# Two of the four weight sums of a down pair: from VectorE additions to accumulating loads issued by GpSimd

## The chip, the cores and the metric

The kernel runs on one core of a Trainium2 chip. The metric is the device time of the program in microseconds. Before the change it is 1649.35 us, the median of three runs (1645.39, 1649.7 and 1649.35). The profiled execution, from which every row below comes, took 1654.24 us.

## The reference

Two layers of a hybrid encoder run on 544 tokens (512 of a first chunk and 32 of a later one) with shared weights. Each layer has two kinds of attention, a cross-attention to 256 memory tokens, and an MLP. The change touches only the second half of the MLP:

```python
hm = rmsnorm(x, norm_mlp[l])                       # x: 544 x 1024
x = x + jnp.square(jax.nn.relu(hm @ w_up[l])) @ w_down[l]   # w_up: 1024 x 4096, w_down: 4096 x 1024
```

Everything is float32, and the kernel keeps that precision by splitting every operand into a high part and a rest (`h` and `lo`) and forming three products.

## The kernel before

The MLP of a layer is done in four groups. A group takes 1024 of the 4096 hidden columns: first eight dense "up" blocks (PE multiplies, VectorE and ScalarE turn the results into activations and their sums), then four "down pairs", each with 128 output rows of the lower and of the upper half of the model width, so a 2 x 2 arrangement of blocks of `w_down` (W11, W21, W12, W22) against the two halves of the tokens and hidden columns. A pair is computed with a Strassen-Winograd scheme: seven products instead of eight, for which four sums of weight blocks are needed besides the four blocks.

`pair()` (line 330) gives each pair its five steps. `load` takes a buffer of seven blocks of 128 x 512 from a ring of two and loads 1 MB in two transfers of 512 KB on SP's queue (line 337). `add(n)` (line 342) is one VectorE addition of 128 x 512. `split(u)` (lines 352 and 353) rounds one or two blocks on ScalarE and subtracts on VectorE; it writes to rings of two (`uh`, `ul`: two blocks) and three (`wh`, `wl`: one block). `product(n)` (line 368) is 12 matmuls. `evac(n)` (line 1085, `evac_pair`) is one VectorE addition that puts a product's PSUM bank on the residual. The sums and the places of the buffer are:

```python
W11, S1, W12, W22, S3, S2, S4 = range(7)
W21 = S1
UNITS = ((W11, 2), (S2, 2), (W12, 1), (S3, 1), (W22, 1))
o, a, b = ((S3, W11, W21), (S1, W21, W22), (S2, S1, W11), (S4, S2, W12))[n]
```

So add 0 is S3 = W11 + W21, add 1 turns W21 in its own place into S1 = W21 + W22, add 2 is S2 = S1 + W11, add 3 is S4 = S2 + W12. Unit 0 (W11 and S1) feeds a pair's first products, unit 1 (S2 and S4) the next.

The order of the 28 products of a group is the table `GROUP`: 0 to 27, with the products of neighbouring pairs interleaved. Products 0, 1, 4, 5, 6, 7, 10 belong to the group's pair 0; 2, 3, 8, 9, 11, 12, 15 to pair 1; 13, 14, 16 to 19, 22 to pair 2; and 20, 21, 23 to 27 to pair 3. Within a pair, the products Q1, N6, Q7 and P4 go to one PSUM bank one after the other, and each is added to what is there, so PE may start Q7 (7, 12, 19, 26) only when VectorE has read the bank after N6 (4, 8, 16, 23), and P4 (10, 15, 22, 27) only after the evacuation of Q7. The pairs take turns in two PSUM buffers, so that pair 2 starts (13) when pair 0's P4 (10) has been read.

`plan()` decides behind which product each load, addition and split is written. The buffer of pair i is free for pair i + 2 when the last split of pair i has been read by VectorE. `mlp()` places the additions of the first two pairs of a group among the up blocks. The tile framework then gives each engine its own order, in which additions and evacuations can change places; the order that counts is the built one, shown with the change.

Of the kernel before, what the change touches and what calls it, by code (L numbers as in the profile page):

```python
# [12 lines left out]
ALU = mybir.AluOpType  # L13
# [41 lines left out]
W11, S1, W12, W22, S3, S2, S4 = range(7)  # L55
W21 = S1
# [32 lines left out]
class Program:  # L89
# [240 lines left out]
    def pair(self, ap, evac):  # L330
# [2 lines left out]

        def load():
            w = st["w"] = self.mlp_pool.tile([128, 7, 512], F32, tag="quad", name="w", bufs=2)
            for c, o in ((0, W11), (1, W12)):
                self.nc.sync.dma_start(out=w[:, o:o + 2].rearrange("p s c -> p (s c)"), in_=ap[c])

        def add(n):
            o, a, b = ((S3, W11, W21), (S1, W21, W22), (S2, S1, W11), (S4, S2, W12))[n]  # L340
            w = st["w"]
            self.nc.vector.tensor_tensor(w[:, o], w[:, a], w[:, b], ALU.add)  # L342

# [1072 lines left out]
    def mlp(self, l, A, goff, bind, at, behind):  # L1416
# [3 lines left out]
        for grp in range(4):  # L1420
            up = [self.dense(io["w_up"][l, 8 * grp + j], 128, *A, bind(self.evac_up, j),
                             ahead=int(n < 7 and (n or not grp))) for n, j in enumerate(PAIRED)]
# [16 lines left out]
        for grp, (up, down) in enumerate(groups):  # L1439
            p0 = HP * grp  # L1440
# [3 lines left out]
            for n in range(8):  # L1444
                j = PAIRED[n]
                late = 2 if grp == 0 and n == 0 else 0
                if n < 7:
                    up[n + 1] = at(up[n + 1], 5 + late, self.rest_up)
                    up[n + 1] = at(up[n + 1], 2 + late, self.sums_up, j)

                if n:
                    up[n] = at(up[n], 8, call, p0 + n // 5, "add", (n - 1) % 4)
                if n == 7:
                    up[n] = at(up[n], 9, call, p0 + 1, "add", 3)
                    up[n] = at(up[n], 1, call, p0, "split", 0)
                    up[n] = at(up[n], 5, call, p0 + 1, "split", 0)
            if grp:
# [15 lines left out]
            for q, (i, n) in enumerate(prods):  # L1473
# [5 lines left out]
                if q:  # L1479
                    i, n = prods[q - 1]  # L1480
                    do(pairs[p0 + i]["evac"], n)
            i, n = prods[q1 - 1]
# [22 lines left out]
    def plan(self, prods, p0, call):  # L1505

        use, free, todo = {}, {}, {}
        for q, (i, n) in enumerate(prods):
            use.setdefault((i, PRODUCTS[n][0]), []).append(q)

        def when(q, i, *a):
            todo.setdefault(q, []).append((call, p0 + i) + a)

        for rank, (ring, units, ahead) in enumerate(RINGS):
            order = sorted((k for k in use if k[1] in units), key=lambda k: use[k][0])
            for n, (i, u) in enumerate(order):
                q = max(use[order[n - ring]][-1] + 1 if n >= ring else 0, use[i, u][0] - ahead)
                assert q < use[i, u][0] or (i, u) == (0, 0)
                free[i] = max(free.get(i, 0), q)
                if u or i > 1:  # L1520
                    todo.setdefault(q + 0.5, []).append((call, p0 + i, "split", u))
        for i in range(HP):
            when(free[i] + 0.7, i + 2, "load")
        for i in (2, 3):
            a, b = [use[i, u][0] - 5 for u in (0, 1)]
            for k, q in enumerate((a - 1, a, b - 1, b)):
                when(max(q, free[i - 2] + 3), i, "add", k)
        return {q: [f for k in sorted(todo) if int(k) == q for f in todo[k]] for q in range(len(prods))}

    def run(self):  # L1530
# [130 lines left out]
```

## Time and profile before

| | |
|---|---|
| median of three runs | 1649.35 us |
| profiled execution: time, and span of its instructions | 1654.24 us, 1652.3 us |
| PE busy | 1602.4 us, 97% of the span |
| VectorE (DVE), ScalarE (ACT), GpSimd (POOL) busy | 1110.5, 800.2 and 313.5 us |
| granted TensorE clock, mean | 0.989 |
| moved by DMA | 157.22 MB, mean 95 GB/s |

The two MLPs take from about 425 to 830 us and from about 1235 us to the end. A line of the timeline is start, duration, engine, source line, operation, output and inputs; in brackets stands the idle time of that engine just before it and the work whose end released it. Rows of neighbouring instructions overlap a little: an engine starts the next when the last one's write is still under way, so the distance between starts is what one costs.

### The profile page before, as it was taken

The numbers are of one execution on the slowest core, as the hardware profiler recorded it, in microseconds if no ns is written. First come the engines' busy times: TensorE is split into PE (matmuls) and PEld (weight loads), VectorE is DVE, ScalarE is ACT, GpSimd is POOL, SyncE is SP. The second block draws the span as 40 slices with busy tenths as digits, with TensorE's granted clock in tenths as the row PEclk, the third lists the DMA queues.
The fourth block names the chain that finished last, engine by engine and source line by source line (L and its number), as shares of the span: only waits on it lengthen the run. The fifth ranks groups of instructions, "written<-read, shape, count | busy, mean of one in ns | idle before, by whom it ended". The sixth has DMA issues, their size and how long they took to land.

```text
span 1652.3 us, 30168 instructions
## 1 busy us (share of the span) xinstructions
PE 1602.4 (97%) x12159; PEld 1512.4 (92%) x12159; DVE 1110.5 (67%) x2135; ACT 800.2 (48%) x1545; POOL 313.5 (19%) x299
## 2 busy tenths in 40 slices
PE   9899999999999999999998999999999999999996
PEld 8777899998999999999987778999989999999996
DVE  6956674355668777776867556634567686867776
ACT  6655564444454444434446555544444434444453
POOL 3524233421300000000244223334212000000003
PEclk9999999999999999999999999999999999999999
DMA  5313156222432223232123112553233223232312
GB/s 164 100 44 110 57 164 175 90 77 68 128 90 90 92 88 103 77 115 74 51 84 101 58 63 89 160 160 90 78 102 91 77 88 105 90 102 78 115 39 80
DMA packets 56395, 157.22 MB, mean 95 GB/s; under 512 B 6768, under 2 KB 16048, under 8 KB 56256
## 3 DMA queue, kind: packets, MB, share of 16 engines
q1 hardware_dynamic: 55984, 155.02, 30.0%
q8 instruction: 95, 1.56, 0.4%
q14 instruction: 44, 0.36, 0.1%
q10 hardware_dynamic: 272, 0.28, 0.0%
HBM read 143.49 MB, written 11.75 MB: 94 GB/s over the span
## 4 chain that ended last, share of the span: by engine, by line
PE 79%; DVE 10%; DMA 4%; ACT 2%; POOL 1%; issue 1%; DVEq 0%; SPq 0%; POOLq 0%; ACTq 0%
PE pd L299 53%; PE pd L368 11%; DMA w<-w_down 2%; PE pw L368 2%; PE pt L474 1%; PE S L641 1%; PE S L573 1%; PE pv L668 1%; PE pv L527 1%; DVE XG L1085 1%; DVE ul L353 1%; PE S L572 1%; PE pv L587 1%; PE S L509 1%; DVE w L342 1%; PE pd L977 1%
## 5 line engine op out<-in xcount | busy, mean ns | idle before, releaser
L299 PE MATMUL pd<-Ah,wl 128*128 128x272 f32 (+2 forms) x2032 | 458.9, 297 | 8.9 <-DVE wl L269 5.4
L299 PE MATMUL pd<-Ah,wh 128*128 128x272 f32 (+2 forms) x2032 | 441.0, 288 | 1.6 <-ACT Ah L410 1.6
L299 PE MATMUL pd<-Al,wh 128*128 128x272 f32 (+2 forms) x2032 | 439.4, 287 | 0.1
L266 ACT CAST wh<-raw 128x512 fp32r<-128x512 f32 (+1 forms) x362 | 221.9, 615 | 303.2 <-PE pd L299 227.1
L299 PEld LDWEIGHTS pd<-Ah,wl 128*128 128x128 f32 (+1 forms) x2032 | 328.7, 189 | 21.7 <-issue 9.6
L299 PEld LDWEIGHTS pd<-Ah,wh 128*128 128x128 f32 (+1 forms) x2032 | 327.8, 189 | 3.1 <-ACT Ah L410 2.6
L299 PEld LDWEIGHTS pd<-Al,wh 128*128 128x128 f32 (+1 forms) x2032 | 328.8, 189 | 0.3 <-DVE Al L411 0.3
L426 POOL TENSOR_TENSOR acc<-acc,sq 128x544 f32<-128x544 f32 x45 | 69.2, 1538 | 806.7 <-ACT sq L425 806.5
L269 DVE TENSOR_TENSOR wl<-raw,wh 128x512 fp32r<-128x512 f32 (+1 forms) x260 | 185.7, 714 | 53.2 <-ACT wh L266 50.8
L269 POOL TENSOR_TENSOR wl<-raw,wh 128x512 fp32r<-128x512 f32 (+1 forms) x102 | 133.2, 1307 | 339.1 <-ACT wh L266 221.3
L352 ACT CAST wh<-w 128x512 fp32r<-128x512 f32 x96 | 59.5, 619 | 142.1 <-PE pw L368 62.0
L299 PE MATMUL pd<-Bh,wl 128*128 128x272 f32 (+1 forms) x576 | 124.4, 295 | 0.7 <-POOL wl L269 0.5
L299 PE MATMUL pd<-Bh,wh 128*128 128x272 f32 (+1 forms) x576 | 121.1, 290 | 0.0
L299 PE MATMUL pd<-Bl,wh 128*128 128x272 f32 (+1 forms) x576 | 121.1, 289 | 0.0
L342 DVE TENSOR_TENSOR w<-w 128x512 f32<-128x512 f32 x128 | 93.2, 730 | 35.7 <-DMA w<-w_down 35.2
L352 ACT CAST uh<-w 128x1024 fp32r<-128x1024 f32 x64 | 67.2, 1051 | 79.3 <-DVE w L342 60.9
L299 PEld LDWEIGHTS pd<-Bh,wl 128*128 128x128 f32 x576 | 90.7, 188 | 3.5 <-issue 1.0
L299 PEld LDWEIGHTS pd<-Bl,wh 128*128 128x128 f32 x576 | 91.1, 189 | 0.3
L299 PEld LDWEIGHTS pd<-Bh,wh 128*128 128x128 f32 x576 | 90.6, 188 | 0.5
L1085 DVE TENSOR_TENSOR XG<-XG,pd 128x272 f32<-128x272 f32 x192 | 80.5, 433 | 13.6 <-PE pd L368 11.8
L353 DVE TENSOR_TENSOR ul<-w,uh 128x1024 fp32r<-128x1024 f32 x64 | 78.1, 1220 | 2.4 <-ACT uh L352 2.4
L1141 DVE SCALAR_TENSOR_TENSOR up<-pd,R 128x544 f32<-128x544 f32 x64 | 46.2, 722 | 45.7 <-PE pd L299 45.7
(309 smaller groups left out, 3219.4 us busy)
## 6 DMA issues: line engine op xcount, KB each, us to landing
w<-w_down SPq DMA_DIRECT2D x64, 512.0 KB, 4.5
raw<-w_up SPq DMA_DIRECT2D x64, 512.0 KB, 3.6
raw<-w_in SPq DMA_DIRECT2D x28, 512.0 KB, 3.4
raw<-w_mk SPq DMA_DIRECT2D x16, 512.0 KB, 3.9
raw<-w_mv SPq DMA_DIRECT2D x16, 512.0 KB, 3.9
raw<-w_out SPq DMA_DIRECT2D x16, 512.0 KB, 3.7
raw<-w_xq SPq DMA_DIRECT2D x16, 512.0 KB, 3.6
raw<-w_xo SPq DMA_DIRECT2D x16, 512.0 KB, 3.6
```

The lines of the kernel that those rows point to most:

```text
L266: nc.scalar.copy(h[:, :n], r)
L269: eng.tensor_tensor(lo[:, :n], r, h[:, :n].bitcast(F32), ALU.subtract)
L299: nc.tensor.matmul(o, w, a[:, c0:c1], start=start and n == 0, stop=stop and n == 2)
L342: self.nc.vector.tensor_tensor(w[:, o], w[:, a], w[:, b], ALU.add)
L352: self.nc.scalar.copy(h, r)
L353: self.nc.vector.tensor_tensor(lo, r, h.bitcast(F32), ALU.subtract)
L368: self.nc.tensor.matmul(st[bank], w[:, c], a, start=first and i == 0 and m == 0, stop=i == HP - 1 and m == 2, skip_group_check=True)
L426: nc.gpsimd.tensor_tensor(self.acc, self.acc, sq, ALU.add)
L474: nc.tensor.transpose(pt[:, j], P[:, j * 128:(j + 1) * 128], self.ident)
L509: nc.tensor.matmul(ps[:, :w], q[hh][:r, i * 128:n], k[hh][:r, :w], start=m == 0, stop=m == 1)
L1085: self.nc.vector.tensor_tensor(x, x, ps, op)
L1141: nc.vector.scalar_tensor_tensor(halves(t), ps[:, :, :HALF], 0.0, halves(self.R), ALU.max, ALU.mult)
```

## The change

W21 is loaded twice, into its own place and into that of S3. Two transfers issued by GpSimd with an addition on the way then put W11 on the second copy (S3) and W22 on the first (S1). VectorE keeps S2 and S4. W21 and W11 are fetched by transfers of 256 KB of their own, W12 and W22 stay in one of 512 KB.

```diff
         def load():
             w = st["w"] = self.mlp_pool.tile([128, 7, 512], F32, tag="quad", name="w", bufs=2)
-            for c, o in ((0, W11), (1, W12)):
-                self.nc.sync.dma_start(out=w[:, o:o + 2].rearrange("p s c -> p (s c)"), in_=ap[c])
+            w11, w21, w12, w22 = [ap[c][:, k:k + 512] for c in range(2) for k in (0, 512)]
+            for o, src in ((S3, w21), (W21, w21)):
+                self.nc.sync.dma_start(out=w[:, o], in_=src)
+            self.nc.sync.dma_start(out=w[:, W11], in_=w11)
+            self.nc.sync.dma_start(out=w[:, W12:W22 + 1].rearrange("p s c -> p (s c)"), in_=ap[1])
+
+            for o, src in ((S3, w11), (S1, w22)):
+                self.nc.gpsimd.dma_start(out=w[:, o], in_=src, accum_op=ALU.add)
 
         def add(n):
-            o, a, b = ((S3, W11, W21), (S1, W21, W22), (S2, S1, W11), (S4, S2, W12))[n]
+            o, a, b = ((S2, S1, W11), (S4, S2, W12))[n]
...
-                if n:
-                    up[n] = at(up[n], 8, call, p0 + n // 5, "add", (n - 1) % 4)
+                if n in (2, 3, 5, 6):
+                    up[n] = at(up[n], 8, call, p0 + n // 5, "add", (n - 2) % 3)
                 if n == 7:
-                    up[n] = at(up[n], 9, call, p0 + 1, "add", 3)
...
         for i in (2, 3):
-            a, b = [use[i, u][0] - 5 for u in (0, 1)]
-            for k, q in enumerate((a - 1, a, b - 1, b)):
-                when(max(q, free[i - 2] + 3), i, "add", k)
+            b = use[i, 1][0] - 5
+            for k, q in enumerate((b - 1, b)):
+                when(max(q, free[i - 2] + 5), i, "add", k)
```

On VectorE, around products 5 to 9 of the first group, the order before is this (w_6120 is the buffer of pair 2, w_5504 that of pair 1; pd_6070 and pw_6166 are PSUM of pair 0, pd_6102 of pair 1):

```order
L353 TENSOR_TENSOR ul_6137<-w_5504,uh_6136 128x1024 [waits Activation_49]
L342 TENSOR_TENSOR w_6120<-w_6120 128x512 [waits DMAHW4_49,DVE_49]
L1085 TENSOR_TENSOR XG_85<-XG_85,pd_6070 128x272 [waits PE_49]
L1085 TENSOR_TENSOR XG_85<-XG_85,pd_6070 128x272 [waits DVE_49]
L1085 TENSOR_TENSOR XG_85<-XG_85,pw_6166 128x272 [waits PE_49]
L342 TENSOR_TENSOR w_6120<-w_6120 128x512 [waits DMAHW5_49]
L353 TENSOR_TENSOR wl_6182<-w_5504,wh_6181 128x512 [waits Activation_49]
L342 TENSOR_TENSOR w_6120<-w_6120 128x512 [waits DVE_49]
L1085 TENSOR_TENSOR XG_85<-XG_85,pd_6070 128x272 [waits PE_49]
L353 TENSOR_TENSOR ul_6217<-w_6120,uh_6216 128x1024 [waits Activation_49]
L353 TENSOR_TENSOR wl_6200<-w_5504,wh_6199 128x512 [waits Activation_49]
L342 TENSOR_TENSOR w_6120<-w_6120 128x512 [waits DVE_49]
```

and now (w_6124 is pair 2's buffer, w_5508 pair 1's, pd_6074 and pd_6106 PSUM of pairs 0 and 1; DMASW is a transfer of GpSimd's, DMAHW one of SP's):

```order
L359 TENSOR_TENSOR ul_6145<-w_5508,uh_6144 128x1024 [waits Activation_49]
L1091 TENSOR_TENSOR XG_85<-XG_85,pd_6074 128x272 [waits PE_49]
L1091 TENSOR_TENSOR XG_85<-XG_85,pd_6074 128x272 [waits DVE_49]
L1091 TENSOR_TENSOR XG_85<-XG_85,pw_6174 128x272 [waits PE_49]
L359 TENSOR_TENSOR wl_6189<-w_5508,wh_6188 128x512 [waits Activation_49]
L348 TENSOR_TENSOR w_6124<-w_6124 128x512 [waits DMAHW2_49,DMASW5_49]
L1091 TENSOR_TENSOR XG_85<-XG_85,pd_6074 128x272 [waits PE_49]
L348 TENSOR_TENSOR w_6124<-w_6124 128x512 [waits DMAHW3_49,DVE_49]
L359 TENSOR_TENSOR wl_6206<-w_5508,wh_6205 128x512 [waits DMASW2_49,Activation_49]
L359 TENSOR_TENSOR ul_6223<-w_6124,uh_6222 128x1024
L1091 TENSOR_TENSOR XG_85<-XG_85,pd_6106 128x272 [waits PE_49]
L1091 TENSOR_TENSOR XG_85<-XG_85,pd_6106 128x272 [waits DVE_49]
```

The first instruction that waits for pair 2's data stood ahead of the evacuations of products 4, 5 and 6; it now stands behind these and ahead of the evacuation of product 7, and it waits for GpSimd's second transfer. On the same engine, where pair 3 comes in, the order before is (w_6252 is pair 3's buffer, w_6120 pair 2's, pd_6294 PSUM of pair 2, pd_6102 of pair 1):

```order
L342 TENSOR_TENSOR w_6252<-w_6252 128x512 [waits DMAHW6_49,DVE_49]
L1085 TENSOR_TENSOR XG_85<-XG_85,pd_6294 128x272 [waits PE_49]
L1085 TENSOR_TENSOR XG_85<-XG_85,pd_6294 128x272
L342 TENSOR_TENSOR w_6252<-w_6252 128x512 [waits DMAHW7_49,DVE_49]
L1085 TENSOR_TENSOR XG_85<-XG_85,pd_6102 128x272 [waits PE_49]
L342 TENSOR_TENSOR w_6252<-w_6252 128x512 [waits DVE_49]
L353 TENSOR_TENSOR wl_6341<-w_6120,wh_6340 128x512 [waits Activation_49]
L353 TENSOR_TENSOR ul_6337<-w_6252,uh_6336 128x1024 [waits Activation_49]
L342 TENSOR_TENSOR w_6252<-w_6252 128x512 [waits DVE_49]
L1085 TENSOR_TENSOR XG_85<-XG_85,pd_6294 128x272 [waits PE_49]
```

and now (w_6258, w_6124, pd_6304 and pd_6106 in their places):

```order
L1091 TENSOR_TENSOR XG_85<-XG_85,pd_6304 128x272 [waits PE_49]
L1091 TENSOR_TENSOR XG_85<-XG_85,pd_6304 128x272
L348 TENSOR_TENSOR w_6258<-w_6258 128x512 [waits DMAHW6_49,DMASW7_49,DVE_49]
L1091 TENSOR_TENSOR XG_85<-XG_85,pd_6106 128x272 [waits PE_49]
L348 TENSOR_TENSOR w_6258<-w_6258 128x512 [waits DMAHW7_49,DVE_49]
L359 TENSOR_TENSOR ul_6345<-w_6258,uh_6344 128x1024 [waits Activation_49]
L359 TENSOR_TENSOR wl_6349<-w_6124,wh_6348 128x512 [waits Activation_49]
L1091 TENSOR_TENSOR XG_85<-XG_85,pd_6304 128x272 [waits PE_49]
```

The waiting addition has moved behind the evacuations of products 13 and 14; behind it stand the evacuation of 15, the second addition, the subtractions of pair 3's unit 0 and of pair 2's last unit, and only then the evacuation of 16. The next pair (the first of the next group, w_6352) is waited for in the same way, between the evacuations of 21 and 22.

GpSimd had no instruction between the last sum of squares ahead of the MLP (line 426, here 432) and the fourth group; its order there is now:

```order
L432 TENSOR_TENSOR acc_5071<-acc_5071,sq_5498 128x544 [waits Activation_49,Pool_49]
L343 DMA w_6124<-w_down 128x512 [waits DMAHW0_49,DMAHW4_49,DMASW1_49,DMAHW5_49,DMASW0_49,DVE_49]
L343 DMA w_6124<-w_down 128x512 [waits DMAHW1_49]
L343 DMA w_6258<-w_down 128x512 [waits DMAHW3_49,DMASW3_49,DMAHW4_49,DMASW2_49,DVE_49]
L343 DMA w_6258<-w_down 128x512 [waits DMAHW5_49]
```

Each pair has gained two transfers there: the one to S3, which waits for the first copy of W21, and the one to S1, which waits for the second copy.

## Rows read from the trace of the kernel before

**Rows 1.** The page's first part: busy time of each engine.
```profile
PE 1602.4 (97%) x12159; PEld 1512.4 (92%) x12159; DVE 1110.5 (67%) x2135; ACT 800.2 (48%) x1545; POOL 313.5 (19%) x299
```

**Rows 2.** Busy time by window, the first group's down stage: PE, PEld, DVE, ACT, POOL.
```profile
503.40:546.80 43.40, 43.17 (x342) 42.62 (x341) 37.13 (x65) 16.88 (x23) 0.00 (x0) 1.00 0.23 76
```

**Rows 3.** What PE's weight loads waited for: us in total, times, longest.
```profile
PEld pd L368 <- DVE XG L1085: 9.4, 16, 1.3
...
PEld pw L368 <- DVE wl L353: 1.1, 1, 1.1
```

**Rows 4.** Timeline of VectorE in that stage: the two additions that wait, and five neighbours.
```profile
513.28 0.69 DVE L342 TENSOR_TENSOR w<-w 128x512 f32<-128x512 f32 x1 [1.25 <-DMA w<-w_down]
...
516.86 0.43 DVE L1085 TENSOR_TENSOR XG<-XG,pd 128x272 f32<-128x272 f32 x1
517.21 1.22 DVE L353 TENSOR_TENSOR ul<-w,uh 128x1024 fp32r<-128x1024 f32 x1
518.35 0.69 DVE L353 TENSOR_TENSOR wl<-w,wh 128x512 fp32r<-128x512 f32 x1
518.95 0.69 DVE L342 TENSOR_TENSOR w<-w 128x512 f32<-128x512 f32 x1
519.55 0.91 DVE L1085 TENSOR_TENSOR XG<-XG,pd 128x272 f32<-128x272 f32 x2
...
526.88 0.69 DVE L342 TENSOR_TENSOR w<-w 128x512 f32<-128x512 f32 x1 [1.55 <-DMA w<-w_down]
```

**Rows 5.** Timeline of PE's weight loads, where product 7 starts: first and last group.
```profile
514.85 0.19 PEld L368 LDWEIGHTS pd<-Bh,wl 128*128 128x128 f32 x1 [0.44 <-DVE XG L1085]
...
1603.15 0.19 PEld L368 LDWEIGHTS pd<-Bh,wl 128*128 128x128 f32 x1 [0.43 <-DVE XG L1085]
```

**Rows 6.** The chain that ended last, in time: start, us, what.
```profile
509.48 3.70 DMA w<-w_down
...
520.87 1.51 PE pw L368 x12
522.38 9.20 PE pd L368 x72
531.59 1.52 PE pw L368 x12
533.10 9.09 PE pd L368 x72
542.19 1.52 PE pw L368 x12
```

**Rows 7.** Timeline of ScalarE: the rounding of two blocks, and of one.
```profile
519.74 1.05 ACT L352 CAST uh<-w 128x1024 fp32r<-128x1024 f32 x1 [2.35 <-DVE w L342]
520.90 0.62 ACT L352 CAST wh<-w 128x512 fp32r<-128x512 f32 x1
```

**Rows 8.** DMA by queue (packets, MB, share), and issues (KB each, median us to landing).
```profile
q1 hardware_dynamic: 55984, 155.02, 30.0%
q8 instruction: 95, 1.56, 0.4%
q14 instruction: 44, 0.36, 0.1%
q10 hardware_dynamic: 272, 0.28, 0.0%
...
w<-w_down SPq DMA_DIRECT2D x64, 512.0 KB, 4.5
...
mem<-memT SPq DMA_DIRECT2D x12, 256.0 KB, 4.3
...
raw<-w_ukv SPq DMA_DIRECT2D x4, 256.0 KB, 2.6
```

**Rows 9.** By tile and line: duration ns min/median/max, first and last start.
```profile
L426 POOL TENSOR_TENSOR acc<-acc,sq x45: 1347/1364/5120, 11.4 to 1620.2; 128x544 f32<-128x544 f32 x45
...
L342 DVE TENSOR_TENSOR w<-w x128: 676/685/1854, 420.8 to 1621.0; 128x512 f32<-128x512 f32 x128
```

**Rows 10.** Timeline of both layers' entries to the MLP: SP, VectorE, then SP, GpSimd, PE.
```profile
415.66 0.80 SPq L337 DMA_DIRECT2D w<-w_down  x2
...
422.13 1.85 DVE L342 TENSOR_TENSOR w<-w 128x512 f32<-128x512 f32 x1
...
1229.97 1.28 SPq L337 DMA_DIRECT2D w<-w_down  x3
...
1233.71 1.30 POOL L269 TENSOR_TENSOR wl<-raw,wh 128x512 fp32r<-128x512 f32 x1 [16.85 <-ACT wh L266]
...
1237.24 0.41 PE L299 MATMUL pd<-Bh,wl 128*128 128x272 f32 x2
```

## The prediction

> **What bounds the kernel now.** I read the page's busy shares first: PE is busy for 1602.4 of 1652.3 us [rows 1], so all that any change off PE can win is in 50 us. The windows then show where these are not: in a group's down stage PE works for 43.17 of 43.40 us, while VectorE works for 37.13 and GpSimd for nothing [rows 2]. VectorE is the second engine there, and the list of what PE waited for names it: the weight loads of the pairs' matmuls (line 368) waited 9.4 us in 16 places for evacuations, and 1.1 us once for a rounding rest [rows 3]. That is the whole stock in the pairs, some 10.5 us or 0.6%. The timeline tells where most of it is made. The first addition of pair 2 holds VectorE for 1.25 us until its load lands [rows 4]; the evacuation of product 4 stands behind it, and product 7 starts 0.44 us late for it [rows 5]. This recurs in all eight groups, with 0.43 us in the last [rows 5]. The first addition of pair 3 waits 1.55 us [rows 4] and PE does not notice. The chain of waits says the same: the load of pair 2 is issued at 509.48 and lands 3.70 us later [rows 6].
>
> So VectorE's busy time is not the bound here. What counts is when a pair's data is ready against the place in VectorE's order where it is waited for, since evacuations stand behind that place.
>
> **The change, part by part.**
>
> *Removed.* 64 of the 128 additions [rows 9]. From start to start one costs 0.60 us (518.95 to 519.55) [rows 4], so 38 us of VectorE's work, almost all beside PE's. With pair 2's first addition moved behind the evacuations of 4, 5 and 6, the 0.44 us at product 7 go: 8 x 0.44 = 3.5 us gained. In the up blocks PE does not wait for these additions, so nothing is gained there.
>
> *Added transfers.* A pair's loads grow from 1 MB to 1.25 MB on SP's queue and 0.5 MB on GpSimd's, 24 MB over the kernel. At a DMA share of 0.23 in this stage [rows 2] the amount costs nothing. GpSimd's own time is free too: it has no work in the first three down stages [rows 2]. In the second layer's entry the transfers stand ahead of one subtraction on GpSimd (1233.71 to 1235.0) whose result PE takes at 1237.24, so 2.2 us of room [rows 10]; the loads were issued at 1229.97, so two issues of under 1 us each after a landing at 1233.7 fit. I take 0; without that cover it is 1 to 2 us once.
>
> *The lengthened chain.* This is the term that decides. Before, pair 2's first addition could start when the first 512 KB had landed: 3.70 us after the issue. Now S1 needs two transfers one after the other: W21's second copy, then the accumulation onto it. W21's copy is the second 256 KB of SP's queue, the same place in the stream as the end of that first 512 KB, so 3.70 us. The accumulation is a transfer of 256 KB through a software queue, and the trace has none: all four queues are hardware or instruction queues [rows 8]. Nearest rows from issue to landing: 2.6 us for w_ukv and 4.3 us for memT, both of 256 KB, and 4.5 us for a w_down of 512 KB [rows 8]. From below S1 is there at 3.7 + 2.6 = 6.3 us after the issue. From above the two accumulations run one behind the other, from the landing of S3's copy, at some 3 us: 3 + 4.5 + 4.5 = 12 us. I take 3.7 + 4.3 = 8.0 us, with memT's duration rather than w_ukv's, because an accumulation also has to read the place that it writes to, and the rest of the pair's load is still under way beside it.
>
> The Trainium skill, DMA: Bandwidth & Descriptors, section "Anatomy of one DMA — SWDGE (gpsimd) path", fits a GpSimd transfer as 2.0 us and its bytes at 436 GB/s, so by estimate 2.6 us here and a chain of 6.3 us, the lower end; no row of before can confirm or deny it.
>
> *Walking the order with 8.0 us*, in the first group, on the trace's clock. Costs from start to start [rows 4]: evacuation 0.35, addition and subtraction of one block 0.60, subtraction of two 1.14; ScalarE's rounding of two 1.05 and of one 0.62 [rows 7]; a product 1.51 [rows 6]. Without the 0.44 us, PE starts product 7 at 514.4, and then, from the chain's times [rows 6] less 0.44, product 10 at 518.9, 13 at 523.5, 19 at 532.7, 22 at 537.2 and 26 at 543.3.
>
> Pair 2: loaded at 509.5, S1 at 517.5. VectorE gets to the addition at 515.7 (evacuation of 6 at 514.45, then a subtraction that waits for its rounding until 515.05), waits 1.8 us, ends it at 518.1 and the evacuation of 7 at 518.45, in time for product 10 (518.9). Then follow an addition, a subtraction, ul, the evacuations of 8 and 9, ul and the last subtraction of pair 1 (0.60 + 0.60 + 1.14 + 0.70 + 1.14 + 0.60): 523.25; the evacuation of 10 ends at 523.6, for product 13 at 523.5. Cost 0.2 us.
>
> Pair 3: that last subtraction frees its buffer, so it is loaded at 523.3, as before (526.88 less 3.70 is 523.2); S1 at 531.3. Behind it: addition 531.9, evacuation of 15 at 532.25, addition 532.85, ul 534.0, subtraction 534.6, evacuation of 16 at 534.95. Product 19, due at 532.9, waits for that one: 2.1 us.
>
> Pair 4 (the next group's first): freed by pair 2's last subtraction, so loaded at 534.65; S1 at 542.65. The evacuation of 21 is done at 537.2 + 2.3 + 0.4 = 539.9, VectorE waits 2.75 us, then addition 543.25, ul 544.9 (its rounding ends at 543.75), evacuation of 22 at 545.25, two subtractions or additions 546.45, evacuation of 23 at 546.8. Product 26, due at 543.3 + 2.3 = 545.6, waits: 1.2 us.
>
> Pair 5 is freed by pair 3's last subtraction at the group's end and is waited for among the up blocks, whose banks have a whole block of room; I take 0. A layer's first pair is loaded at 415.7 and would be complete at 423.7, while VectorE gets to its first addition at about 422; it waits 1.7 us there and is spared two additions of up to 1.85 us each [rows 10]. PE has the wide output blocks to work on meanwhile; I take 0, and 2 us a layer if they don't cover it.
>
> So a group costs 0.2 + 2.1 + 1.2 - 0.44 = 3.1 us, and a layer's last group, which has no pair 4, 0.2 + 2.1 - 0.44 = 1.9 us. Sum: 6 x 3.1 + 2 x 1.9 = 22 us. The profiled execution takes 1654.2 us and would take 1676; the median lies 4.9 us under it, so I forecast 1671 us.
>
> *How steep this is.* The same walk with 7.0 us gives no wait at 10 and 13, 0.25 at 19 and 0.25 at 26: with the gain, 0 in all. With 9.0 us: 0.3 + 0.6 at 10 and 13, 3.3 at 19, 2.3 at 26, so 6.1 a group and 3.8 in the last, 44 us. With 10.0 us 9.1 and 5.8, 66 us. Beyond 7 us each further microsecond of the chain costs 22 us, because it is paid at pair 3, passed on to the issue of pair 4's load, and paid there again. At 6.3 us only the gain is left, -3.5 us.
>
> **The rivals.**
>
> *The chain is short and nothing changes.* The accumulation takes 2.6 to 3.5 us, as w_ukv's row has it, and the chain 6.3 to 7.2 us: -3.5 to +5 us, 1646 to 1654. For it: the two transfers can be issued before SP's last one has landed, and this stage's DMA queues are empty for three quarters of the time [rows 2]. Against it: memT's loads of the same size took 4.3 us [rows 8]. The formula of the Trainium skill that is named above would land here, at 1646.
>
> *Faster.* The chain stays under 6.2 us, so that it ends before VectorE gets to the addition, and the relief of VectorE takes the other waits of the pairs along, those of the fourth groups and of the tail: up to 10.5 us [rows 3], typically 6 to 8, so about 1642. The point that decides is 515.7 - 509.5 = 6.2 us. For it: VectorE is busy at 86% here [rows 2] and loses 0.6 us an addition. Against it: it needs an accumulation faster than any row of 256 KB.
>
> *GpSimd is held up by VectorE.* On its usual 1.36 us, GpSimd's addition of sums took up to 5.12 us in the trace, and VectorE's additions, usually 0.69, up to 1.85 where they met [rows 9]: the two hold each other up when they work from the same memory. If the writing of descriptors waits for VectorE in the same way, each of the two issues of a pair is put off by up to one VectorE instruction (0.6 to 1.1 us), and the chain is 9 to 10 us: +44 to +66 us, 1693 to 1715. Against it: over 45 such additions the median stayed at 1.36 us [rows 9]. An accumulation that is slow in itself ends at the same price. The Trainium skill, SBUF — State Buffer, section "SBUF: two separate sides", describes such a case: while VectorE holds the port that the two share, GpSimd cannot write its descriptors and its transfer stands still; that the two delay each other the trace shows, that it reaches descriptors no row here can show.
>
> **How the numbers follow.** Chances: forecast (chain 7.2 to 8.7 us, 1654 to 1687, likeliest 1671) 0.42; short chain, no change 0.20; faster 0.10; held up or slow 0.28. About 0.3% or 5 us is what can be told from no change here: faster by more 0.10, within 0.20, slower by more 0.70. The range leaves out the upper part of the last case and the lower of the faster one: 1643 to 1698, which is a chain of about 6 to 9.3 us.
>
> **What would show it.** GpSimd's transfers appear with a software queue of their own, 64 issues of 256 KB, and a landing time: about 4.3 us right, under 3.5 or over 5 us wrong. VectorE's waits for additions must change from a transfer of SP's to one of GpSimd's, 1.8 us at pair 2, about 3 us at pairs 3 and 4, and PE's waits for evacuations must move from product 7 to 19 and 26 and grow from 9.4 to some 30 us. If VectorE waits there and PE does not, the room that I gave the evacuations of 16 and 23 is wrong; if PE's time is lost in the up blocks, it is pair 5 that I costed at nothing.

## The result, and the profile after

The changed kernel takes 1748.45 us (median of six runs, 1740.34 to 1757.33) against 1650.21 us for the kernel before: ratio 1.0582, 95% interval 1.0559 to 1.0605. That is 98 us more where 22 were forecast. The direction was right, and so was the place where most of it is lost; the size was not, and the range ended 50 us too low.

The page after, its first part, shows PE's share down from 97% [rows 1] to 93%. PE stands still for 114.9 us of the span instead of 49.9, and its busy time for the same 12159 matmuls has grown by 34.5 us. VectorE has the relief that the change was to give (1110.5 to 1065.9 us) and nothing comes of it.

```profile
PE 1636.9 (93%) x12159; PEld 1541.3 (88%) x12159; DVE 1065.9 (61%) x2071; ACT 795.9 (45%) x1545; POOL 363.5 (21%) x363
```

The queues and the issues on the same page (to compare with [rows 8]): GpSimd's transfers have a software queue of their own, 64 of 256 KB, and take 5.7 us from issue to landing.

```profile
q0 software_dynamic: 9216, 16.78, 6.1%
...
w<-w_down POOLq DMA_DIRECT2D x64, 256.0 KB, 5.7
```

The list of waits (us in total, times, longest), in answer to [rows 3]: the waits of PE's weight loads for evacuations in the pairs go from 9.4 to 56.1 us. Behind them stand VectorE's waits for a transfer of GpSimd's, 123.6 us, and ScalarE's for the same data, 172.5 us. In the kernel before the same list had 35.2 us for VectorE, in 23 places. The last three lines are the idle time of the matmuls themselves: 49.0 and 6.7 us in the pairs (line 374) and 23.4 us in the dense blocks (line 299), where the kernel before had 5.7, 0 and 5.4.

```profile
ACT uh L358 <- DMA w<-w_down: 172.5, 30, 10.7
DVE w L348 <- DMA w<-w_down: 123.6, 32, 7.1
PEld pd L374 <- DVE XG L1091: 56.1, 32, 6.1
...
PE pd L374 <- DVE XG L1091: 49.0, 26, 5.9
PE pd L299 <- DVE wl L269: 23.4, 13, 3.7
PE pd L374 <- DVE ul L359: 6.7, 2, 4.4
```

Before:

```profile
DVE w L342 <- DMA w<-w_down: 35.2, 23, 2.4
...
PE pd L368 <- DVE XG L1085: 5.7, 12, 1.1
PE pd L299 <- DVE wl L269: 5.4, 4, 1.5
```

VectorE's timeline in the first group's down stage and the next up blocks has the four additions that begin a pair's sums, in answer to [rows 4]. The brackets are VectorE's wait: 3.45 us at pair 2, 5.49 at pair 3, 0.97 at pair 4, 5.30 at pair 5. The line ahead of pair 4's is an evacuation, for which VectorE waited 2.87 us for PE.

```profile
524.69 0.69 DVE L348 TENSOR_TENSOR w<-w 128x512 f32<-128x512 f32 x1 [3.45 <-DMA w<-w_down]
...
540.71 0.69 DVE L348 TENSOR_TENSOR w<-w 128x512 f32<-128x512 f32 x1 [5.49 <-DMA w<-w_down]
...
552.35 0.78 DVE L1091 TENSOR_TENSOR XG<-XG,pd 128x272 f32<-128x272 f32 x2 [2.87 <-PE pd L374]
554.10 0.69 DVE L348 TENSOR_TENSOR w<-w 128x512 f32<-128x512 f32 x1 [0.97 <-DMA w<-w_down]
...
571.93 1.42 DVE L348 TENSOR_TENSOR w<-w 128x512 f32<-128x512 f32 x2 [5.30 <-DMA w<-w_down]
```

The chain of waits takes the stretch before the first two of them apart (start, us, what; compare [rows 6]). At pair 2: the first copy of W21 lands 2.54 us after the issue, GpSimd gets to its first transfer (S3's) at 518.27, that issue takes the place of S1's for 0.52 us, and S1's own transfer lands 5.81 us later. From load to addition that is 9.72 us (514.97 to 524.69). At pair 3 the load's first issue is at 530.75; the second copy of W21 starts at 531.12 and takes 3.83 us, S1's issue begins 0.40 us after it, and its transfer takes 5.29: 9.96 us (530.75 to 540.71).

```profile
514.97 2.54 DMA w<-w_down
...
518.27 0.52 POOL w L343
...
518.86 5.81 DMA w<-w_down
...
531.12 3.83 DMA w<-w_down
...
535.35 5.29 DMA w<-w_down
```

Where PE stops behind the second of them, PE's weight loads show 4.77 us (to compare with the 0.44 us of [rows 5]). It is product 19, waiting for the evacuation of 16, as forecast. PE's matmuls lose 4.55 us there, and in the same group 1.40 ahead of product 10, 0.32 ahead of 13 and 0.65 ahead of 26.

```profile
544.96 0.29 PEld L374 LDWEIGHTS pd<-Bh,wl 128*128 128x128 f32 x1 [4.77 <-DVE XG L1091]
```

The windows of 4 us around that place (busy time and instructions of PE, PEld, DVE, ACT, POOL, then granted clock, DMA share and GB/s) show what no term of the prediction had. After the stop the clock is 0.50: 1.2 instead of 2.4 GHz. In the next 4 us PE finishes 18 matmuls instead of 34, in the 4 us behind that 27. After the two shorter stops earlier in the group (525 to 533, 1.40 and 0.32 us) the clock stays at 1.00.

```profile
525.00:529.00 4.00, 3.21 (x24) 3.04 (x24) 3.96 (x8) 2.98 (x4) 0.00 (x0) 1.00 0.00 0
529.00:533.00 4.00, 3.68 (x28) 3.43 (x28) 3.97 (x7) 1.24 (x2) 0.00 (x0) 1.00 0.27 100
...
541.00:545.00 4.00, 0.04 (x1) 0.04 (x1) 3.97 (x8) 2.92 (x4) 0.00 (x0) 0.86 0.01 2
545.00:549.00 4.00, 4.00 (x18) 4.00 (x19) 2.65 (x5) 0.62 (x1) 1.55 (x2) 0.50 0.87 251
549.00:553.00 4.00, 4.00 (x27) 4.00 (x27) 1.13 (x3) 0.00 (x0) 0.21 (x1) 0.79 0.98 200
553.00:557.00 4.00, 4.00 (x34) 4.00 (x33) 2.51 (x5) 1.57 (x2) 0.00 (x0) 1.00 0.07 12
```

One window from the first product of a group to the first of the next sums this up, first in the kernel before, then after. 90.83 us became 103.04. PE's idle time went from 0.22 to 8.57 us (+8.4), and its busy time, for 722 and 723 matmuls, from 90.61 to 94.47 us (+3.9).

```profile
503.54:594.37 90.83, 90.61 (x722) 90.05 (x721) 68.52 (x114) 38.67 (x54) 0.00 (x0) 1.00 0.29 94
```

```profile
509.04:612.08 103.04, 94.47 (x723) 93.06 (x721) 63.73 (x106) 38.04 (x54) 7.05 (x8) 0.97 0.43 113
```

### The profile page after: what moved, and what is told of

It is laid out like the page before. It is cut to its first block, busy times and chain, and to the rows that moved or that the text cites. A ratio compares the mean times of both kernels' runs of the same rounds, so it can differ in the third digit from the quotient of the medians.

```text
span 1751.8 us, 30433 instructions
## 1 busy us (share of the span) xinstructions
PE 1636.9 (93%) x12159; PEld 1541.3 (88%) x12159; DVE 1065.9 (61%) x2071; ACT 795.9 (45%) x1545; POOL 363.5 (21%) x363
## 3 DMA queue, kind: packets, MB, share of 16 engines
q0 software_dynamic: 9216, 16.78, 6.1%
## 4 chain that ended last, share of the span: by engine, by line
PE 59%; DMA 16%; DVE 13%; issue 5%; POOL 2%; ACT 2%; SPq 0%; POOLq 0%; DVEq 0%; ACTq 0%
PE pd L299 44%; DMA w<-w_down 15%; DVE ul L359 3%; PE pd L374 3%; DVE XG L1091 2%; PE pt L480 1%; PE S L579 1%; DVE wl L359 1%; DVE w L348 1%; PE S L647 1%; PE pv L533 1%; DVE wl L269 1%; PE pv L674 1%; PE S L578 1%; POOL w L343 1%
## 5 line engine op out<-in xcount | busy, mean ns | idle before, releaser
L343 POOL DMA_DIRECT2D w<-w_down x64 | 56.8, 996 | 717.0 <-DMA w<-w_down 406.2
L358 ACT CAST uh<-w 128x1024 fp32r<-128x1024 f32 x64 | 67.0, 1047 | 200.8 <-DMA w<-w_down 172.5
L348 DVE TENSOR_TENSOR w<-w 128x512 f32<-128x512 f32 x64 | 44.5, 695 | 123.8 <-DMA w<-w_down 123.6
L432 POOL TENSOR_TENSOR acc<-acc,sq 128x544 f32<-128x544 f32 x45 | 63.2, 1404 | 155.2 <-ACT sq L431 154.9
L374 PE MATMUL pd<-Bh,wl 128*128 128x272 f32 x128 | 42.8, 334 | 47.1 <-DVE XG L1091 47.1
```

What stands on the lines that cost most here:

```text
L343: self.nc.gpsimd.dma_start(out=w[:, o], in_=src, accum_op=ALU.add)
L358: self.nc.scalar.copy(h, r)
L374: self.nc.tensor.matmul(st[bank], w[:, c], a, start=first and i == 0 and m == 0, stop=i == HP - 1 and m == 2, skip_group_check=True)
L432: nc.gpsimd.tensor_tensor(self.acc, self.acc, sq, ALU.add)
```

## The experiments

The theory: S1 is complete too late, VectorE waits for it ahead of evacuations, PE stops, and a long stop also lowers PE's clock. The rival that mattered most: the accumulating transfers cost by being there, because GpSimd and VectorE hold each other up or because of the memory traffic.

**S3 alone.**

```diff
+            self.nc.sync.dma_start(out=w[:, S3], in_=ap[0][:, 512:])
+            self.nc.gpsimd.dma_start(out=w[:, S3], in_=ap[0][:, :512], accum_op=ALU.add)
...
-            o, a, b = ((S3, W11, W21), (S1, W21, W22), (S2, S1, W11), (S4, S2, W12))[n]
+            o, a, b = ((S1, W21, W22), (S2, S1, W11), (S4, S2, W12))[n]
```

> One part of the change alone: only S3 is formed by an accumulating load (W21 loaded a second time into S3's place, W11 added to it by GpSimd's transfer); S1, S2 and S4 are VectorE's, and a pair's four blocks are loaded as before. S3 is needed only by unit 3, some ten products after unit 0, so nothing waits for the accumulation on VectorE ahead of an evacuation. Theory (the whole loss is the wait of VectorE for the S1 that is complete too late): 1645 to 1653 us, no wait of VectorE or ScalarE for a transfer longer than before. Rival 1 (the accumulating transfers cost by being there: memory traffic, GpSimd and VectorE holding each other up): half of the 98 us, about 1700 us.

Measured: 1655.99 us against 1652.65, ratio 1.0024 (1.0013 to 1.0036). Half of the transfers cost 3 to 4 us and not 50. The theory's figure is missed by 3 us: the removed additions gave nothing back, and a small loss that no row places is left over. Product 7 does not wait in the first group any more, but other products do: PE's weight loads wait 8.9 us for evacuations in the pairs, before 9.4.

**S1 alone.**

```diff
-            for o, src in ((S3, w11), (S1, w22)):
+            for o, src in ((S1, w22),):
...
-            o, a, b = ((S2, S1, W11), (S4, S2, W12))[n]
+            o, a, b = ((S2, S1, W11), (S4, S2, W12), (S3, S3, W11))[n]
```

> The other part of the change alone: S1 by an accumulating load, S3 added by VectorE in its place after S2 and S4 (W21 is loaded twice as in the changed kernel). GpSimd issues one transfer per pair. Theory (S1's chain is the whole loss): the chain is that of the changed kernel less one issue of 0.88 us and less the company of the second accumulation, 8.5 to 9 us, and the time 1700 to 1735 us. Rival 1 (the two accumulations cost by being there, half each): about 1700 us, with S3's share as seen in the kernel with S3 alone then missing.

Measured: 1722.48 us, ratio 1.0430 (1.0417 to 1.0444), as the theory had it. One accumulation per pair costs 70 us as S1 and 3 to 4 as S3, so S1's place in the chain makes the loss, not the number of accumulations. The run is not the chain alone: its built order has S3's addition, which waits for a load of SP's, ahead of the one that waits for S1. VectorE's waits at pairs 2 and 3 show both, and the later of each two ends 8.70 and 8.61 us after its load (512.26 and 527.55):

```profile
518.03 0.69 DVE L348 TENSOR_TENSOR w<-w 128x512 f32<-128x512 f32 x1 [1.18 <-DMA w<-w_down]
520.96 0.69 DVE L348 TENSOR_TENSOR w<-w 128x512 f32<-128x512 f32 x1 [1.28 <-DMA w<-w_down]
...
533.28 0.69 DVE L348 TENSOR_TENSOR w<-w 128x512 f32<-128x512 f32 x1 [3.51 <-DMA w<-w_down]
536.16 0.69 DVE L348 TENSOR_TENSOR w<-w 128x512 f32<-128x512 f32 x1 [1.14 <-DMA w<-w_down]
```

**S1 first.**

```diff
-            for o, src in ((S3, w21), (W21, w21)):
+            for o, src in ((W21, w21), (S3, w21)):
...
-            for o, src in ((S3, w11), (S1, w22)):
+            for o, src in ((S1, w22), (S3, w11)):
```

> The changed kernel with the two accumulations and their first copies in the other order: S1's copy of W21 is loaded first and W22 added to it by GpSimd's first transfer, S3 comes second. Theory (chain from the load's issue to S1): S1's accumulation no longer stands behind the issue of S3's (0.88 us), so the chain goes from about 10 to about 9.1 us; at 22 us of PE idleness per us of chain, and another half of that for the granted clock, about 1720 us (1705 to 1730). Rival 1 (cost by being there): unchanged, 1748 us.

Measured: 1728.78 us, ratio 1.0469 (1.0445 to 1.0492). The chain got shorter than expected (8.1 us at pair 2, 8.6 at pair 3), the time only as expected. The framework built another order on VectorE here, in which pair 4's two additions stand together ahead of two evacuations and wait 2.9 us, so this run is no pure measure of the chain's length.

**The same transfers, not accumulating.**

```diff
-                self.nc.gpsimd.dma_start(out=w[:, o], in_=src, accum_op=ALU.add)
+                self.nc.gpsimd.dma_start(out=w[:, o], in_=src)
```

> The changed kernel with GpSimd's two transfers of a pair as plain copies onto the same places, not accumulating (so two sums of weights are left out of the computation); number, size, order and waits of the transfers are the same. Sub-theory A (adding on the way is what makes the transfer take 5.7 us): the landing falls to 2.6 to 4.3 us, the chain to 7 to 8.5 us, the time to 1655 to 1690 us. Sub-theory B (any transfer that GpSimd issues takes so long): landing 5.7 us, 1748 us.

Measured: 1698.93 us, ratio 1.0276 (1.0245 to 1.0307), with the order of VectorE unchanged. That is between the two sub-theories and 9 us above A's range: the addition on the way is worth 50 us, and a plain GpSimd transfer is still late enough to cost 46. The chain is 7.8 us at pair 2 and 8.6 at pair 3. The instructions of line 343 (ns min/median/max, and us to landing) show both parts: the issue falls from 0.885 to 0.536 us, the landing from 5.7 to 4.0.

```profile
L343 POOL DMA_DIRECT2D w<-w_down x64: 536/536/722, 419.4 to 1654.9; - x64
...
DMA to landing us min/median/max: 3.0/4.0/6.9
```

In the changed kernel the same lines read:

```profile
L343 POOL DMA_DIRECT2D w<-w_down x64: 856/885/1256, 418.1 to 1710.2; - x64
...
DMA to landing us min/median/max: 3.6/5.7/8.4
```

And the queue's row of the plain run, for the same 16.78 MB, has 5120 packets and a share of 2.8%, where the accumulating transfers had 9216 and 6.1%.

```profile
q0 software_dynamic: 5120, 16.78, 2.8%
```

The Trainium skill, Collectives: The Full Stack, section "The bandwidth ceiling: the fold count and why AG ≠ RS ≠ AR", says of the addition in a collective's ReduceScatter that it makes the transfer slow because it needs two source reads, not because the adding takes time. For the accumulating load the rows agree in direction (1.8 times the packets, 2.2 times the queue's share); no run here separates the two.

**Plain, and S1 first.** Both edits above together.

> The changed kernel with S1's transfers ahead of S3's, and GpSimd's transfers plain instead of accumulating (two sums of weights are left out of the computation). The order on all engines is that of the kernel with S1 first, which took 1729 us. The chain is 2.5 us for the copy, 0.7 us to GpSimd's issue and 4.0 us for the plain transfer: 7.2 us. Theory (beyond some 7 us each us costs 22 us of idle PE and half as much in clock): 1655 to 1680 us. Rival (the second transfer as such, a fixed price): within 10 us of the kernel with plain transfers and S3 first, 1690 to 1710 us.

Measured: 1700.21 us, ratio 1.0303 (1.0285 to 1.0321): the theory's figure is missed, the rival's met. The chain was 7.7, 7.4 and 7.2 us at pairs 2 to 4, and VectorE still waited 2.3, 2.9 and 2.4 us, since in this built order it arrives earlier at pairs 2 and 4 (5.4 and 4.9 us after the load) and pair 4's additions stand ahead of two evacuations. The rival's reason, a fixed price of the second transfer, does not hold beyond this run: in two runs further down both transfers are there and cost 2 and 5 us. So "7 us cost nothing" holds at best for the order that it was worked out on.

**The transfers aside, a first try.**

```diff
+            aside = [self.mlp_pool.tile([128, 512], F32, tag="aside", name="aside", bufs=2) for _ in range(2)]
+            for x in aside:
+                self.nc.sync.dma_start(out=x, in_=ap[0][:, 512:])
+            for c, x in enumerate(aside):
+                self.nc.gpsimd.dma_start(out=x, in_=ap[c][:, 512 * c:512 * c + 512], accum_op=ALU.add)
```

> The kernel before, with all its additions on VectorE, and beside it per pair two further loads of W21 and two accumulating transfers by GpSimd of the same sizes as in the changed kernel, onto tiles that nothing reads. So all the transfers of the change are there and nobody waits for them. Theory: 1648 to 1658 us. Rival 1 (the transfers cost by being there): most of the 98 us is back, 1700 us or more.

Measured: 1739.01 us, ratio 1.0530 (1.0512 to 1.0547). It looks like the rival's case and is not. Since nothing depends on the tiles, the framework put the transfers of many pairs one behind the other into SP's queue. SP's timeline shows that: 4 of them over 10.31 us ahead of the next pair's load, which leaves only at 551.97. VectorE waits 16.09 us for it:

```profile
541.55 10.31 SPq L340 DMA_DIRECT2D aside<-w_down  x4
551.97 0.84 SPq L337 DMA_DIRECT2D w<-w_down  x2
```

```profile
556.00 0.69 DVE L347 TENSOR_TENSOR w<-w 128x512 f32<-128x512 f32 x1 [16.09 <-DMA w<-w_down]
```

**The transfers aside, tied to the pair's buffer.**

```diff
-            w = st["w"] = self.mlp_pool.tile([128, 7, 512], F32, tag="quad", name="w", bufs=2)
+            w = st["w"] = self.mlp_pool.tile([128, 8, 512], F32, tag="quad", name="w", bufs=2)
...
+            self.nc.sync.dma_start(out=w[:, 7], in_=ap[0][:, 512:])
+            for c in range(2):
+                self.nc.gpsimd.dma_start(out=w[:, 7], in_=ap[c][:, 512 * c:512 * c + 512], accum_op=ALU.add)
```

> The kernel before, all its additions on VectorE and in its own order, and beside it per pair one further load of W21 (256 KB, SP) and two accumulating transfers by GpSimd (256 KB each) onto an eighth place of the same pair's buffer, which nothing reads. The transfers of the change are there, in the stage where the change has them, and nobody waits for them but the buffer's next load. Theory (what is waited for costs, not the transfers): 1648 to 1660 us. Rival 1 (the transfers cost by being there, by the memory or the port that GpSimd and VectorE share): the base loads and VectorE's additions get longer and the time is 1690 us or more.

Measured: 1655.31 us, ratio 1.0015 (1.0005 to 1.0025). All the traffic and all of GpSimd's issues are there, and the loss is 2 us. The rival falls, as far as one accumulation at a time goes; two side by side come with the run after this one. VectorE's additions keep their 0.684 us median. Here the two accumulations of a pair run one after the other, and each lands in 4.3 us:

```profile
L340 POOL DMA_DIRECT2D w<-w_down x64: 856/872/1199, 427.2 to 1627.3; - x64
...
DMA to landing us min/median/max: 3.5/4.3/7.9
```

In the run with S3 alone it was 3.9 us, in that with S1 alone 4.6, and 5.7 only where two run side by side.

**The change with the chain hidden, and its control.** A ring of three buffers of five blocks, with S2 written over W11 and S4 over S1 once unit 0 has been rounded, lets each pair be loaded one pair earlier. The additions' places move with it.

```diff
-W11, S1, W12, W22, S3, S2, S4 = range(7)
-W21 = S1
+W11, S1, W12, W22, S3 = range(5)
+W21 = S4 = S1
+S2 = W11
...
-            w = st["w"] = self.mlp_pool.tile([128, 7, 512], F32, tag="quad", name="w", bufs=2)
+            w = st["w"] = self.mlp_pool.tile([128, 5, 512], F32, tag="quad", name="w", bufs=3)
...
-            when(free[i] + 0.7, i + 2, "load")
+            when(free[i] + 0.7, i + 3, "load")
```

> The changed kernel, both sums by accumulating loads, with a ring of three buffers of five blocks instead of two of seven: S2 is written over W11 and S4 over S1, both after unit 0 has been rounded, so that a pair can be loaded one pair earlier. The chain of some 10 us from load to S1 then has 15 to 20 us until VectorE asks for it. Theory (the chain costs only where it is waited for): 1645 to 1660 us, no wait of VectorE for a transfer of a pair in a down stage, granted clock back at 0.99. Rival 1 (accumulating transfers cost by being there): 1690 us or more. Gain over the kernel before, if the relief of VectorE were worth something: below 1645 us.

> The same ring of three buffers of five blocks with the kernel before, all four additions on VectorE: the control for the run with accumulating loads. The wait of the first addition of pair 2 goes, and with it 0.4 us of PE in each of eight groups: 1645 to 1653 us.

Measured: with accumulating loads 1656.69 us, ratio to the kernel before 1.0029 (1.0015 to 1.0044); the control 1650.42 us, ratio 0.9989 (0.9974 to 1.0004). The accumulations, two side by side as in the change, land as late as ever (5.7 us), and 93 of the 98 us are gone. With accumulating loads, VectorE's additions in the down stage have no bracket any more:

```profile
520.22 1.41 DVE L349 TENSOR_TENSOR w<-w 128x512 f32<-128x512 f32 x2
532.61 1.41 DVE L349 TENSOR_TENSOR w<-w 128x512 f32<-128x512 f32 x2
```

The control's expectation holds for the time and not for the reason. Its first addition in the first down stage still waits 1.17 us, for a load issued 3.7 us earlier, and product 7 still waits 0.36 us. PE's weight loads wait 7.3 us for evacuations in the pairs; with accumulating loads it is 3.3 us, first that run, then the control:

```profile
PEld pd L375 <- DVE XG L1092: 3.3, 5, 1.2
```

```profile
PEld pd L369 <- DVE XG L1086: 7.3, 14, 1.3
```

No version of the change beats the kernel before, and the control is not told from it.

**The entry of a layer.** `vec` is true for the first two pairs of a layer.

```diff
-            for o, src in ((S3, w11), (S1, w22)):
+            for o, src in () if vec else ((S3, w11), (S1, w22)):
...
```

> The changed kernel with the two pairs that a layer's MLP begins with summed by VectorE as before; the other 28 pairs by accumulating loads. Theory (the entry costs some 5 us a layer that were forecast at 0, the rest is the down stages): 1735 to 1743 us. If the entry cost nothing: 1748 us.

Measured: 1737.49 us, ratio 1.0513 (1.0480 to 1.0546), in the theory's range; against the changed kernel that is 11 us less, by the two intervals some 5 to 18 us. In the first layer PE has no idle time any more in the 90 us ahead of the first products, where the changed kernel has 5.09 us; first this run, then the changed kernel:

```profile
410.00:500.00 90.00, 90.00 (x708) 89.20 (x708) 62.95 (x91) 43.55 (x69) 11.97 (x8) 1.00 0.33 102
```

```profile
410.00:500.00 90.00, 84.91 (x651) 83.68 (x650) 52.27 (x78) 39.66 (x63) 14.42 (x12) 0.98 0.42 118
```

In the second layer a stop of 3.71 us is gone. The theory that the rest is the down stages as they were is not what the whole span shows: PE's idle time did not fall (115.5 us against 114.9; the waits in the pairs grew from 55.7 to 60.6), and its busy time did, from 1636.9 to 1620.0 us, with a mean clock of 0.981 against 0.970. How the 11 us divide stays open.

**PE kept busy ahead of product 19.**

```diff
+        ps = self.ps_s.tile([128, 512], F32, tag="s", name="fill")
+        for _ in range(24):
+            self.nc.tensor.matmul(ps[:, :256], self.mask[:, 1], self.mask[:, 1:3], start=True, stop=True)
```

> The changed kernel with 24 matmuls of 256 columns, on a constant and into a bank that nothing reads, ahead of product 19 of every group, the place where PE stood still for some 4 us and then ran at half its clock for some 6 us. As a side effect pair 4's additions move ahead of two evacuations. Theory (a part of the loss is not waiting but the clock that falls behind a wait): the clock behind the place stays at 1.0, 23 us come back in spite of the added work, 1720 to 1735 us. Rival (PE's longer matmuls come from something else, memory for one): clock and time as in the changed kernel or above, 1748 to 1770 us.

Measured: 1797.44 us, ratio 1.0876 (1.0851 to 1.0901), a miss in the sum. The clock did as the theory says at the filled place (first two windows), but pair 4's additions, now ahead of two evacuations, made a new stop of over 4 us behind it, and the clock fell there (0.57):

```profile
541.00:545.00 4.00, 2.83 (x22) 2.83 (x23) 3.52 (x7) 0.84 (x2) 0.23 (x1) 1.00 0.58 184
545.00:549.00 4.00, 3.45 (x28) 3.23 (x26) 0.00 (x0) 0.00 (x0) 1.53 (x2) 1.00 0.87 225
549.00:553.00 4.00, 0.00 (x0) 0.00 (x0) 2.12 (x4) 1.56 (x2) 0.00 (x0) 1.00 0.27 49
553.00:557.00 4.00, 3.47 (x16) 3.48 (x17) 2.56 (x5) 0.00 (x0) 0.00 (x0) 0.57 0.02 4
```

**A stop of PE without any late weights.**

```diff
+                if q in (18, 19):
+                    do(self.stall, q == 18)
...
+        if not start:
+            self.nc.tensor.matmul(ps[:, :256], self.mask[:, 1], self.late[:, :256], start=True, stop=True)
+            return
+        self.nc.tensor.matmul(ps[:, :256], self.mask[:, 1], self.mask[:, 1:3], start=True, stop=True)
+        t = self.late = self.mlp_pool.tile([128, 544], BF16, tag="late", name="late", bufs=1)
...
+        self.nc.scalar.copy(t[:, :256], ps[:, :256])
+        for _ in range(4):
+            self.nc.gpsimd.tensor_tensor(t[:, :512], t[:, :512], t[:, :512], ALU.add)
```

> The kernel before, with a wait of PE of its own making in each of the eight groups: ahead of product 19 a matmul of 256 columns into an unread bank needs a tile that ScalarE copies behind product 17 and on which GpSimd, idle in this stage, then makes four additions of 128 x 512. Nothing of the weights waits. By GpSimd's 1.36 us for an addition of 544 columns PE stands still for some 4 us a group, 34 us in all. Theory (a wait of this length costs its own time and then a lower granted clock): the clock falls to half behind each, PE's busy time grows by a third to a half of the idle time, 1700 to 1715 us. Rival (PE's longer matmuls in the changed kernel come from the accumulating transfers): PE's busy time grows by 2 us at most, the clock stays, 1682 to 1690 us.

Measured: 1688.82 us, ratio 1.0228 (1.0211 to 1.0245). The stops came out at 3.5 us in seven groups, 24.5 us in all instead of 34, so the time lies where the rival's was put; the rows decide for the theory. PE's busy time grew by 16.4 us (1602.4 to 1618.8). The 16 added matmuls take some 5 us of that themselves (0.28 and 0.33 us each), so the others grew by some 11.5 us and not by 2. The clock behind the first stop is 0.62, and in the 4 us behind each of the other six it is 0.50 to 0.64:

```profile
533.00:537.00 4.00, 1.45 (x11) 1.28 (x11) 3.74 (x4) 0.94 (x2) 3.77 (x4) 1.00 0.40 162
537.00:541.00 4.00, 3.16 (x15) 3.16 (x15) 1.65 (x3) 0.62 (x1) 1.34 (x2) 0.62 0.00 0
541.00:545.00 4.00, 4.00 (x33) 4.00 (x32) 3.28 (x7) 1.49 (x2) 0.00 (x0) 0.95 0.00 0
```

```profile
PE stall L1503 <- POOL late L1510: 24.5, 7, 3.5
```

So of the 39 us that the kernel takes longer some 5 are the added matmuls, and 24.5 us of stops cost some 34 us, with no accumulating transfer in the kernel.

## Why the prediction was wrong

*Direction and the first two places: right.* The change costs only through the lengthened chain: with the chain hidden 1.0029 is left, with the transfers unread 1.0015. VectorE waits at pairs 2 and 3, and PE in front of product 19, as the walk had it.

*Added transfers: right in the down stages.* The amount was taken at 0, and the run with an unread place shows 2 us for it. The issues of "under 1 us each" take 0.885 in the median and 1.256 at most.

*The lengthened chain: the term that was mis-sized.* 8.0 us were forecast, 9.7 and 10.0 measured. Its second summand failed, the accumulation at 4.3 us by memT's row. That is near right for an accumulation by itself: 3.9 with S3 alone, 4.3 one after the other, 4.6 with S1 alone. But a pair's two run side by side, and then they take 5.7, which the prediction's own sign ("over 5 us wrong") calls a miss. The waits on GpSimd were not in the sum either. At pair 2 it needs 0.76 us from the landing to its first issue, and S3's issue takes another 0.59; there this is nearly paid for by the first copy of W21, which lands in 2.54 us rather than 3.7. At pair 3 the second copy lands 4.2 us after the load and S1's issue follows 0.40 us later. The case for a longer chain was on record with 0.28 ("slow in itself", 9 to 10 us), and it should have been the bound of the range. The lower rival had 2.6 us for a transfer, by w_ukv's row and by the fit of the Trainium skill, DMA: Bandwidth & Descriptors, section "Anatomy of one DMA — SWDGE (gpsimd) path"; even the plain transfers, two side by side, took 4.0, so here the measurement decides against the fit.

*The walk: right at pairs 2 and 3, wrong at pair 4.* For a chain of 10.0 us it gave 9.1 us a group: 6.2 ahead of products 10, 13 and 19, less the gain of 0.44, and 3.3 ahead of product 26 for pair 4. In the six groups that have a pair 4, PE's matmuls lost 5.9 to 8.7 us ahead of the first three, 6.3 in the group shown, but only 0.65 ahead of 26 there and 1.94 at most. The loss "paid there again" did not come in this form: VectorE came to pair 4's addition late itself, after 2.87 us of waiting for products that PE worked off at the lower clock, so that 0.97 us were left to wait.

*The sum of the idle time: right by luck.* The walk's 66 us for 10.0 us of chain meet the 65 us by which PE's idle time grew. But in the pairs PE's waits grew by some 50 us (5.7 to 49.0 and 6.7); the entries add 8.8 us and the up blocks 9.4, which the prediction had at 0, and other places lose some 3 us less than before. The steepness of 22 us per us fits the plain run, with a chain of 7.8 to 8.6 us and 27.7 us more idle time (77.6 of its span of 1693.4 us, against 49.9). It does not fit the runs with S1 first and with S1 alone: for their 8.1 to 8.7 us it gives 24 to 37 us, and their idle time grew by 53.6 and 52.8. Their built orders on VectorE are others, as is that of the run with plain transfers and S1 first; so the walk's threshold of 7 us and its slope belong to one order.

*A term that was missing: the clock.* The walk counted a stop at its length. PE's busy time grew by 34.5 us in the changed kernel, 22.9 with S1 first, 16.9 with S1 alone and 13.4 with plain transfers, 0.32 to 0.53 of the growth of idle time, and by some 11.5 us behind 24.5 us of stops of another make. By these shares, an estimate, the forecast's own 22 us would have been 29 to 34.

*Layer entry and pair 5: costed at 0, wrong.* PE stands still for 5.09 us in the first layer's entry and 3.71 in the second's, where the price without cover was put at 2 us a layer; without accumulating loads there the kernel takes 11 us less. VectorE's first addition waits 7.14 us in the trace (to 427.28) where 1.7 were walked. At pair 5, costed at nothing because "a whole block of room" was to cover it, VectorE waits 5.30 us, and PE loses 1.65 us in the up block there (573 to 577 us: 2.35 of 4.00 us busy); in all six such places it is 1.2 to 1.9 us.

*GpSimd held up by VectorE: not the cause.* The issues took 856 to 1256 ns with a median of 885, and VectorE's additions 691. At pair 3 VectorE stood still from 535.2 to 540.71, all through the issue and the transfer of S1 (535.35, 5.29 us), and S1 was as late as elsewhere. The case that the Trainium skill, SBUF — State Buffer, section "SBUF: two separate sides", describes is not what these rows show.

*The removed additions: worth nothing in the time.* With S3 alone and in the run with the chain hidden, product 7 no longer waits in the first group. With S3 alone other products wait instead; with the chain hidden PE's waits for evacuations do fall, from 9.4 to 3.3 us, and the time does not (1.0029). The control can't speak to it, since its product 7 still waits. What makes the kernels with S3 alone, with the unread place and with three buffers and accumulating loads 0.15 to 0.3% slower stays open; PE's idle and busy time in their profiled executions don't place it.

## What to carry to other kernels

When work moves from an engine to a transfer, price the moment at which its result is there, not the engine time that it frees: an engine with slack gave nothing back here, and a wait in front of evacuations is paid by PE. Two dependent transfers are priced from issue to landing with everything that runs beside them, their own twin first. A stop of PE of several us is to be counted with the clock behind it, in these runs a third to a half as much again. And when a forecast's total meets the measured one, its parts are to be compared place by place before the model is believed.

## What was not expected of the hardware

An accumulating transfer of 256 KB from GpSimd takes 0.885 us of GpSimd to issue (a plain one 0.536) and 144 packets (80), lands in 3.9 to 4.6 us by itself and in 5.7 beside a second one. Stops of PE of 3.5 us were followed by a granted clock of 0.50 to 0.64 over 4 us, one of 4.55 us by 0.50. The length alone does not decide: in the changed kernel a stop of 2.22 us was followed by 0.58 over 4 us (from 857.22), one of 2.46 us by 1.00 (from 629.89).
